# Weight sums in DRAM through one queue, squares on another engine: a one-core encoder layer on Trainium2

## The chip, the cores and the metric

The kernel runs on one core of a Trainium2 chip. A core has five engines that run side by side, each with its own instruction queue in order: TensorE (PE, matrix products; its weight loads appear as PEld), VectorE (DVE), ScalarE (ACT), GpSimd (POOL) and SyncE (SP). Transfers between DRAM and the on-chip memory, or within DRAM, are run by 16 DMA engines that all queues share. SP issues them through a queue that the profile calls q1 (hardware_dynamic), GpSimd through q0 (software_dynamic); a transfer that adds to what is at its destination ("accumulate") goes through GpSimd here. The metric is the time of one execution in microseconds (us) of device time; lower is better.

## The reference

One layer of a bidirectional encoder on x of 512 tokens by 1024 channels, in float32. First comes token mixing: RMSNorm, one wide input projection whose columns feed a two-way Mamba-2 scan, windowed attention and two gates; the branches are merged and projected, normed and added. Then comes channel mixing, the part that the change touches:

```python
h = rmsnorm(x, pre_mlp_norm[l])
f = jnp.square(jax.nn.relu(h @ w_mlp_in[l])) @ w_mlp_out[l]
x = x + rmsnorm(f, post_mlp_norm[l])
```

w_mlp_in is 1024 by 4096 and w_mlp_out 4096 by 1024.

## The kernel before, in words

Every float32 operand is split in two: hi, which ScalarE rounds to TensorE's faster float32 format (a CAST), and lo, the rest, which VectorE or GpSimd subtracts. A product is then three matmuls (mm3, line 418, recorded at line 412). Splits of weights are at line 492 (ScalarE) and 500 (VectorE or GpSimd) for most weights, at 1766 and 1770 for w_mlp_out and w_o; of activations at 429 to 433.

The work is a list of quanta, each a set of matmuls with the weights that it needs. The input projections, scan and attention take the first 629 us or so, the scan's output projection and the mixing until 756, the MLP the rest. The hidden width of 4096 is cut into four parts of 1024. Part 0 of the up projection is a plain product (up_halves, up_quantum). Then the down projection of part p (7 quanta) is interleaved with the up projection of part p + 1 (16 quanta); part 3 of the down projection comes last. Down part 0 starts at 803.8 us, part 1 at 885, part 2 at 969 and part 3 at 1051.9.

The up projections of parts 1 to 3 and all four down projections are folded: a 2 by 2 block product with seven block products instead of eight, after Strassen and Winograd. That needs four sums of blocks on each side. On the side of the weights they are made in one of two ways:

- **By transfer** (sums_in_dram, line 1451): a block is copied to a scratch tensor in DRAM and other blocks are accumulated on it, in eight transfers of 1 MB (four copies and four accumulations, copy after accumulation where one sum starts from another). Before the change the copies are issued by SP (line 1462) and the accumulations by GpSimd (line 1460). SUMS (line 41) says which parts do this and when: a first quantum and a pace in quanta. The numbers from 80 up count from 100 at the start of the MLP. Up parts 1, 2 and 3 (scratch up1s, up2s, up3s) are made during the scan, down parts 2 and 3 (dn2s, dn3s) during the MLP. The weights then come in finished: 28 loads of 256 KB for a down part.
- **On the core** (fold, lines 1737 to 1745): the down projection loads 16 raw blocks of 256 KB and VectorE makes the sums, 16 additions of 128x512 (lines 1728 and 1729). Down parts 0 and 1 do this.

The up projection's output is squared after a relu, by square (line 1570), 48 times in parts 1 to 3 (four products in four units of each part): ScalarE takes the relu into a tile r or q (line 1572), and VectorE multiplies max(a, 0), or min(a, 0), with it (line 1573). Where the folded product has the opposite sign, relu is taken of -a and the result is the negative of the square; combine (line 1646), which makes the operands of the down projection, takes that sign into account through its argument.

The order of the instructions on each engine is fixed when the program is made, by the class Planner: a model of the engines with a cost for each instruction (duration, line 210) and a due time worked back from the matmul that needs it (deadlines, line 245). It takes the ready instruction that is due first. For transfers it assumes 1 us of GpSimd for an issue, 125 bytes per ns on GpSimd's queue, and loads that are 1.6 times slower while that queue is busy (SOFT and SLOW, line 39). The transfers of the sums are also held back until the matmul issued before them in the program has started (held_back, line 1364). SP and GpSimd run their instructions in the planned order: if one waits, all behind it on that engine wait too.

Of the kernel before, what the change touches and what calls it, by code (L numbers as in the profile page):

```python
# [12 lines left out]
AF = mybir.ActivationFunctionType  # L13
ALU = mybir.AluOpType
# [23 lines left out]
HEADS = dict(scores=0, flip=2, values=3.5)  # L38
SOFT, SLOW = 125, 1.6
FETCH, STAGE, HALF = 2, 1, 3  # L40
SUMS = dict(up={1: (10, 2), 2: (26, 2), 3: (42, 2)}, down={2:(104,3),3:(130,3)})
BUCKET_STARTS = (1, 2, 3, 4, 5, 6, 7, 8, 12, 16, 23, 32, 46, 64, 91)


# [16 lines left out]
class Slots:  # L61
# [5 lines left out]
    def get(self, name, shape=(128, 512), dtype=F32):  # L67
        s = self.free.popleft()
        self.n += 1
        t = self.pool.tile(list(shape), dtype, tag=f"s{s}", name=f"{name}_{self.n}", bufs=1)  # L70
        self.tags[t.tensor.name] = f"s{s}", 1
        self.slot[id(t)] = (s, t)
        return t

    def put(self, *tiles):
        for t in tiles:
            self.free.append(self.slot.pop(id(t))[0])
# [275 lines left out]
class Trunk:  # L353
# [1097 lines left out]
    def sums_in_dram(self, name, src, q, pace):  # L1451

        nc = self.nc
        t = [self.dp.tile([512, 512], F32, name=f"{name}s{i}") for i in range(1, 5)]

        def step(out, a, plus):
            def run():
                a_ = t[a] if isinstance(a, int) else src(*a)
                if plus:
                    nc.gpsimd.dma_start(t[out], a_, accum_op=ALU.add)  # L1460
                else:
                    nc.sync.dma_start(t[out], a_)
            return run

        steps = [(0, (0, 0), False), (0, (0, 1), True), (2, (0, 1), False), (2, (1, 1), True),
                 (1, 0, False), (1, (1, 1), True), (3, 1, False), (3, (1, 0), True)]
        for i, args in enumerate(steps):
            self.at(q + pace * i, lambda fn=step(*args): self.held_back(fn))
        return t
# [77 lines left out]
    def up_unit(self, part, k):  # L1547

        nc = self.nc
        get, put = self.slots.get, self.slots.put  # L1550
        lo, hi = slice(0, 256), slice(256, 512)
        bank, made = {}, {}

        def block(n):
            return self.ups[part][n][:, k * 128:(k + 1) * 128].rearrange("(k p) n -> p k n", p=128)

        def product(w, b, at, first):
            ps, cols = bank[at[0]], at[1]
            for i in range(4):
                self.mm3(ps[:, cols], (w[0][:, i], w[1][:, i]), self.bt[b][i], first and i == 0, i == 3, not first)  # L1560

        def copy(n, at):
            made[n] = get(n, (128, 256))
            nc.scalar.copy(made[n], bank[at[0]][:, at[1]])

        def plus(at, a, n):
            nc.vector.tensor_tensor(bank[at[0]][:, at[1]], bank[a[0]][:, a[1]], made[n], op=ALU.add)
            put(made.pop(n))

        def square(at, r, side, dst=None):  # L1570
            a, cols = bank[at[0]], at[1]
            nc.scalar.activation(r[:, cols], a[:, cols], AF.Relu, scale=1.0 if side == ALU.max else -1.0)
            nc.vector.scalar_tensor_tensor((dst or a)[:, cols], a[:, cols], 0.0, r[:, cols], op0=side, op1=ALU.mult)
            if side == ALU.min:
                put(r)

        X, Y, Z, V = (1, lo), (0, hi), (0, lo), (1, hi)

        def one(w):
            bank[1] = self.bank("pp")  # L1580
            product(w[0], "B11", X, True)
            copy("c0", X)
            bank[0] = self.bank("pp")
            product(w[1], "T1", Y, True)
            copy("cy", Y)

        def two(w):
            product(w[0], "T2", X, False)
            copy("c1", X)
            product(w[1], "B21", Z, False)  # L1590
            plus(Z, Z, "c0")
            made["r"] = get("r")
            square(Z, made["r"], ALU.max)
            self.operand(part, k, bank[0][:, lo])

        def three(w):
            product(w[0], "T3", X, False)
            plus(V, X, "cy")
            square(V, get("q"), ALU.min)
            product(w[1], "B22", Y, False)  # L1600
            plus(Y, Y, "c1")
            square(Y, made["r"], ALU.max, made["r"])

        def four(w):
            product(w[0], "T4", X, False)
            square(X, get("q"), ALU.min)
            self.pair = [bank[0][:, lo], made["r"][:, hi], made["r"], bank[1]]
            self.combine(part, k, -1.0)

        def quantum(names, run, eng):  # L1610
            def go(parts):
                h, l = parts[0]
                run([(h[:, 4 * j:4 * j + 4], l[:, 4 * j:4 * j + 4]) for j in range(len(names))])
            return Quantum([([block(n) for n in names], 4 * len(names), 128, eng)], go)

        return [quantum(("A11", "S1"), one, UP_LO[0]), quantum(("S2", "A12"), two, UP_LO[1]),
                quantum(("S3", "S4"), three, UP_LO[2]), quantum(("A22",), four, UP_LO[3])]

    def up_done(self, ps, i):
# [23 lines left out]
        f["A12"] = self.halves(self.f12)[k % 2]  # L1643
        self.held[part].extend([{"A22": fa}] + [{"A12": self.f12}] * (k % 2))

    def combine(self, part, k, sign=None):

        nc = self.nc
        get, put = self.slots.get, self.slots.put
        a11, a21, r, b = self.pair  # L1650
        self.pair = []
        f = self.f[part, k]
        lo, hi = slice(0, 256), slice(256, 512)
        tt = nc.vector.tensor_tensor
        s, t = get("fs"), get("ft")
        fs, ft = self.twin("fs"), self.twin("ft")
        if sign is None:
            self.operand(part, k, a11)
            tt(t[:, lo], a21, b[:, hi], op=ALU.subtract)
        else:  # L1660
            tt(t[:, lo], a21, b[:, hi], op=ALU.add)
        tt(s[:, lo], t[:, lo], a11, op=ALU.subtract)
        tt(s[:, hi], a11, a21, op=ALU.subtract)
        put(r)
        self.split(*fs, s)
        if sign is None:
            tt(t[:, hi], b[:, lo], s[:, lo], op=ALU.add)
        else:
            tt(t[:, hi], s[:, lo], b[:, lo], op=ALU.subtract)
        self.split(*f["A22"], b[:, hi], sign)  # L1670
        self.split(*ft, t)
        self.split(*f["A12"], b[:, lo], sign)
        put(s, t)
        (f["S2"], f["S3"]), (f["S1"], f["S4"]) = self.halves(fs), self.halves(ft)
        self.held[part].extend([{"S3": fs}, {"S4": ft}])
# [181 lines left out]
    def build(self):  # L1857
# [11 lines left out]
        self.ups, self.dnt = {}, {}  # L1869
        for p, at in SUMS["up"].items():  # L1870
            if at[0] < 80:
# [35 lines left out]
        self.at(n() + 3, self.token_sums)  # L1907
        for p, at in SUMS["up"].items():
            if at[0] >= 80:
                self.ups[p] = self.up_blocks(p, n() + at[0] - 100, at[1])  # L1910
        for p, at in SUMS["down"].items():
            self.dnt[p] = self.down_sums(p, n() + at[0] - 100, at[1])
# [44 lines left out]
```

## Time and profile before

| | |
|---|---|
| median of 3 runs | 1100.24 us (1099.0 to 1104.58) |
| the profiled execution's own time | 1103.85 us |
| its span, first to last instruction | 1101.6 us |
| mean granted clock of TensorE | 0.993 |
| instructions | 18311 |

The times are those of whole executions; the profile is of one more execution, whose span of 1101.6 us lies within its own time of 1103.85 us. A row of the profile names a line of the program, the engine, the operation, the tile that is written and those that are read, the shapes and the count, and then the busy time in us and the mean duration of one in ns. After a second bar stand the idle time of that engine just before these instructions and what ended it. "SPq" is SP's queue of transfers, "POOLq" GpSimd's. A row of the chain of waits gives a start, a length and what the end of the program was waiting for at that time. A row of waits gives who waited for whom: the sum in us, how many times, and the longest.

### The profile page before, as it was taken

What the parts mean: (1) busy time and instruction counts of PE and PEld (TensorE: products, weight loads), DVE (VectorE), ACT (ScalarE), POOL (GpSimd) and SP (SyncE); (2) the same over time, 40 slices, a digit from 0 to 9 for tenths busy, and PEclk for the clock granted to TensorE, in tenths of its full rate; (3) what the DMA queues carried; (4) which work ended last, traced back from release to release, by engine and by line L of the source; (5) the groups of instructions that cost most, each with busy time, mean ns of one, the idle gap of its engine ahead of it and who ended that gap; (6) DMA issues with size and microseconds to landing.
All of it is one profiled execution on the core that took longest, in us unless ns stands there. A gap on an engine that the chain in (4) does not pass through costs nothing.

```text
span 1101.6 us, 18311 instructions
## 1 busy us (share of the span) xinstructions
PE 1074.3 (98%) x6016; PEld 915.6 (83%) x6016; DVE 838.7 (76%) x1471; ACT 695.3 (63%) x1515; POOL 814.4 (74%) x1003
## 2 busy tenths in 40 slices
PE   8999999999899999999999999999999999999997
PEld 7888888888778888888888888888888888988885
DVE  6568678699388687788778457769999798756867
ACT  5567676686577767576777522477867555646653
POOL 4447567568467799999898777666989888858753
PEclk9999999999989999999999999999999999999999
DMA  7458739868758776966664479844767599697673
GB/s 221 124 139 223 187 87 230 199 173 211 182 127 221 183 228 151 257 157 185 179 150 107 125 244 315 262 154 136 228 162 183 176 281 266 170 253 214 195 223 116
DMA packets 260016, 209.98 MB, mean 191 GB/s; under 512 B 14478, under 2 KB 214646, under 8 KB 259761
## 3 DMA queue, kind: packets, MB, share of 16 engines
q1 hardware_dynamic: 249212, 187.77, 58.5%
q0 software_dynamic: 10560, 20.97, 11.6%
q8 instruction: 47, 0.77, 0.3%
q14 instruction: 49, 0.39, 0.1%
q10 hardware_dynamic: 148, 0.07, 0.0%
HBM read 195.86 MB, written 54.85 MB: 228 GB/s over the span
## 4 chain that ended last, share of the span: by engine, by line
PE 61%; DVE 9%; DMA 3%; ACT 3%; issue 2%; SPq 1%; POOL 0%; POOLq 0%; DVEq 0%; ACTq 0%
PE pp L412 44%; PE ps L412 16%; DMA wd<-dn2s 2%; DVE wd L1729 1%; DMA rf<-csT 1%; PE ps L416 1%; DVE wl L500 1%; DMA wd<-in_w_mlp_out 1%; DVE fsl L430 1%; DVE acc L1816 1%; ACT P L887 0%; DVE wt L1728 0%; DVE ftl L430 0%; ACT m L1136 0%; DVE P L893 0%
## 5 line engine op out<-in xcount | busy, mean ns | idle before, releaser
L500 POOL TENSOR_TENSOR wl<-wr,wh 128x256 fp32r<-128x256 f32 (+1 forms) x503 | 427.4, 882 | 137.4 <-ACT wh L492 128.4
L412 PE MATMUL pp<-b,wh 128*128 128x512 f32 (+1 forms) x1840 | 519.3, 366 | 4.7 <-DVE fal L430 2.5
L412 PEld LDWEIGHTS pp<-b,wh 128*128 128x128 f32 x1840 | 330.3, 189 | 62.1 <-DVE fal L430 3.5
L412 PE MATMUL pp<-b,wl 128*128 128x512 f32 (+1 forms) x920 | 336.8, 366 | 1.3 <-DVE wl L500 1.3
L492 ACT CAST wh<-wr 128x1024 fp32r<-128x1024 f32 (+1 forms) x155 | 156.5, 1009 | 80.6 <-PE pp L412 46.6
L412 PEld LDWEIGHTS pp<-b,wl 128*128 128x128 f32 x920 | 173.7, 189 | 29.8 <-DVE wl L500 1.9
L1770 POOL TENSOR_TENSOR wl<-wd,wh 128x256 fp32r<-128x256 f32 x168 | 140.2, 863 | 49.6 <-ACT wh L1766 27.8
L1766 ACT CAST wh<-wd 128x512 fp32r<-128x512 f32 x124 | 72.6, 618 | 40.9 <-PE ps L412 13.0
L500 DVE TENSOR_TENSOR wl<-wr,wh 128x256 fp32r<-128x256 f32 x78 | 56.8, 744 | 9.4 <-ACT wh L492 9.1
L1135 ACT ACTIVATE n<-cb,tables 128x128 f32<-128x128 f32 x128 | 49.9, 392 | 19.9 <-DVE cb L1126 19.3
L967 DVE SCALAR_TENSOR_TENSOR u<-pp,cv,u 128x510 f32<-128x510 f32 (+1 forms) x64 | 47.7, 746 | 13.3 <-ACT u L963 11.9
L1136 ACT ACTIVATE m<-cb,tables 128x128 f32<-128x128 f32 x128 | 49.7, 391 | 1.2 <-DVE cb L1126 1.2
L1131 ACT ACTIVATE rf<-rf,tables 128x128 f32<-128x128 f32 x128 | 41.9, 393 | 13.4 <-DMA rf<-csT 13.0
L1171 POOL TENSOR_TENSOR w<-w,E 128x256 f32<-128x256 f32 x48 | 39.6, 840 | 7.1 <-DVE w L1167 5.9
L887 ACT ACTIVATE P<-P,mx 128x384 f32<-128x384 f32 (+1 forms) x64 | 35.2, 552 | 13.8 <-DVE mx L884 13.8
L1065 POOL TENSOR_TENSOR xd<-x,tables 128x256 f32<-128x256 f32 x48 | 33.9, 729 | 12.9 <-ACT x L990 12.2
L1129 POOL TENSOR_TENSOR rb<-rb,tables 128x512 f32<-128x512 f32 x32 | 34.2, 1075 | 12.0 <-DMA rb<-csT 8.6
L1816 DVE TENSOR_TENSOR acc<-acc,ps 128x512 f32<-128x512 f32 (+1 forms) x49 | 32.6, 668 | 12.2 <-PE ps L412 12.2
L878 DVE CUSTOM_DVE_ANT_0 P<-ps,bt,sink 128x256 f32<-128x256 f32 (+1 forms) x64 | 31.9, 545 | 10.4 <-PE ps L412 9.9
L1770 DVE TENSOR_TENSOR wl<-wd,wh 128x512 fp32r<-128x512 f32 x40 | 31.6, 797 | 10.3 <-ACT wh L1766 9.2
L1095 POOL TENSOR_TENSOR pv<-pv,tables 128x256 f32<-128x256 f32 x32 | 24.5, 778 | 16.6 <-DVE pv L1096 10.3
L1132 DVE TENSOR_TENSOR rf<-rf,rb 128x512 f32<-128x512 f32 x32 | 31.0, 970 | 4.4 <-POOL rb L1129 4.4
(338 smaller groups left out, 2503.8 us busy)
## 6 DMA issues: line engine op xcount, KB each, us to landing
wr<-in_w_in SPq DMA_DIRECT2D x74, 512.0 KB, 5.1
wd<-in_w_mlp_out SPq DMA_DIRECT2D x56, 256.0 KB, 5.0
wr<-in_w_mlp_in SPq DMA_DIRECT2D x36, 256.0 KB, 4.1
rb<-csT SPq DMA_DIRECT2D x32, 256.0 KB, 5.7
rf<-csT SPq DMA_DIRECT2D x32, 256.0 KB, 6.8
wr<-in_w_ssd_out SPq DMA_DIRECT2D x14, 512.0 KB, 4.8
wd<-in_w_o SPq DMA_DIRECT2D x28, 256.0 KB, 5.6
E<-csE SPq DMA_DIRECT2D x96, 64.0 KB, 4.4
```

The lines of the kernel that those rows point to most:

```text
L412: self.nc.tensor.matmul(out, lhsT, rhs, start=start, stop=stop, skip_group_check=more)
L492: self.nc.scalar.copy(hi[:, :m], raw)
L500: engines[e].tensor_tensor(lo[:, c], raw[:, c], hi[:, c].bitcast(F32), op=ALU.subtract)
L887: nc.scalar.activation(p[:, :w], p[:, :w], AF.Exp, bias=mx[:, n:n + 1], accum_out=sm[:, n:n + 1])
L967: nc.vector.scalar_tensor_tensor(u[:, a:e], ps[:, a + d:e + d], self.wtap(t, b), u[:, a:e], op0=ALU.mult, op1=ALU.add)
L1131: nc.scalar.activation(v4(rf)[:, h], v4(rf)[:, h], AF.Identity, bias=ncs[:, 0, h:h + 1])
L1135: nc.scalar.activation(v4(n)[:, h], cb[:, 0], AF.Copy, scale=dt[:, 0, h:h + 1])
L1136: nc.scalar.activation(v4(m)[:, h], cb[:, 1], AF.Copy, scale=dt[:, 1, h:h + 1])
L1171: nc.gpsimd.tensor_tensor(wc, wc, E[:, d], op=ALU.add)
L1766: nc.scalar.copy(hi, w)
L1770: (nc.vector if e == "v" else nc.gpsimd).tensor_tensor(low[:, q], w[:, q], hi[:, q].bitcast(F32), op=ALU.subtract)
L1816: self.nc.vector.tensor_tensor(self.acc[t, j][:, c], self.acc[t, j][:, c], ps[:, c], op=ALU.subtract if minus else ALU.add)
```

## The change

Four things are changed. The copies of sums_in_dram are issued by GpSimd, like the accumulations. The sums of up part 3 are made at the start of the MLP and not during the scan, and down part 2 makes its sums on the core, so that four sets of eight transfers are left of five. The squares are a relu and a Square, both on ScalarE. All squares are now positive, so the sign in combine goes away.

```diff
-SUMS = dict(up={1: (10, 2), 2: (26, 2), 3: (42, 2)}, down={2:(104,3),3:(130,3)})
+SUMS = dict(up={1: (10, 2), 2: (26, 2), 3: (102, 3)}, down={3:(130,3)})
...
         def step(out, a, plus):
             def run():
                 a_ = t[a] if isinstance(a, int) else src(*a)
-                if plus:
-                    nc.gpsimd.dma_start(t[out], a_, accum_op=ALU.add)
-                else:
-                    nc.sync.dma_start(t[out], a_)
+                nc.gpsimd.dma_start(t[out], a_, **(dict(accum_op=ALU.add) if plus else {}))
             return run
...
-        def square(at, r, side, dst=None):
+        def square(at, r, scale, dst=None):
             a, cols = bank[at[0]], at[1]
-            nc.scalar.activation(r[:, cols], a[:, cols], AF.Relu, scale=1.0 if side == ALU.max else -1.0)
-            nc.vector.scalar_tensor_tensor((dst or a)[:, cols], a[:, cols], 0.0, r[:, cols], op0=side, op1=ALU.mult)
-            if side == ALU.min:
+            nc.scalar.activation(r[:, cols], a[:, cols], AF.Relu, scale=scale)
+            nc.scalar.activation((dst or a)[:, cols], r[:, cols], AF.Square)
+            if scale < 0:
                 put(r)
...
-            square(Z, made["r"], ALU.max)
+            square(Z, made["r"], 1.0)
...
-            square(V, get("q"), ALU.min)
+            square(V, get("q"), -1.0)
...
-            square(Y, made["r"], ALU.max, made["r"])
+            square(Y, made["r"], 1.0, made["r"])
...
-            square(X, get("q"), ALU.min)
+            square(X, get("q"), -1.0)
             self.pair = [bank[0][:, lo], made["r"][:, hi], made["r"], bank[1]]
-            self.combine(part, k, -1.0)
+            self.combine(part, k, False)
...
-    def combine(self, part, k, sign=None):
+    def combine(self, part, k, whole=True):
...
-        if sign is None:
+        if whole:
             self.operand(part, k, a11)
-            tt(t[:, lo], a21, b[:, hi], op=ALU.subtract)
-        else:
-            tt(t[:, lo], a21, b[:, hi], op=ALU.add)
+        tt(t[:, lo], a21, b[:, hi], op=ALU.subtract)
...
-        if sign is None:
-            tt(t[:, hi], b[:, lo], s[:, lo], op=ALU.add)
-        else:
-            tt(t[:, hi], s[:, lo], b[:, lo], op=ALU.subtract)
-        self.split(*f["A22"], b[:, hi], sign)
+        tt(t[:, hi], b[:, lo], s[:, lo], op=ALU.add)
+        self.split(*f["A22"], b[:, hi])
         self.split(*ft, t)
-        self.split(*f["A12"], b[:, lo], sign)
+        self.split(*f["A12"], b[:, lo])
```

## The prediction

> **What bounds the kernel now.** I read the head of the page first, then busy time by stage, then the chain of waits, then the DMA queues. The head says whose time this is.
>
> ```profile
> span 1101.6 us, 18311 instructions
> PE 1074.3 (98%) x6016; PEld 915.6 (83%) x6016; DVE 838.7 (76%) x1471; ACT 695.3 (63%) x1515; POOL 814.4 (74%) x1003
> ```
>
> TensorE is idle for 1101.6 - 1074.3 = 27.3 us in all. The change leaves every matmul as it is, so 27.3 us is the most that it can win, and what it can lose is new idle time of TensorE. The windows view, with one row for a stretch (PE, PEld, DVE, ACT, POOL busy, then granted clock, DMA share, GB/s), shows where the idle time lies.
>
> ```profile
> core 0: us, PE busy (x) PEld busy (x) DVE busy (x) ACT busy (x) POOL busy (x), PEclk, DMA share, GB/s
> 0.00:50.00 50.00, 46.65 (x252) 39.38 (x253) 30.65 (x61) 27.73 (x55) 21.56 (x37) 1.00 0.64 181
> 250.00:350.00 100.00, 94.91 (x575) 79.31 (x574) 73.00 (x158) 63.77 (x156) 65.57 (x85) 0.97 0.72 180
> 803.80:885.00 81.20, 78.59 (x481) 70.44 (x480) 70.83 (x110) 50.26 (x95) 72.40 (x87) 0.98 0.64 179
> 885.00:969.00 84.00, 80.78 (x506) 71.55 (x505) 69.72 (x126) 47.03 (x92) 69.69 (x81) 1.00 0.94 242
> 969.00:1052.00 83.00, 79.58 (x508) 71.98 (x507) 59.70 (x113) 49.84 (x97) 60.32 (x74) 1.00 0.69 204
> 1075.00:1101.60 26.60, 18.49 (x92) 15.45 (x90) 20.19 (x39) 10.16 (x26) 10.38 (x12) 0.90 0.29 108
> 336.00:500.00 164.00, 164.00 (x891) 136.79 (x890) 128.04 (x189) 115.93 (x268) 147.25 (x179) 1.00 0.78 201
> ```
>
> The first 50 us and the tail hold 3.3 + 8.1 us; no edit is there. Parts 0, 1 and 2 of the MLP (the rows that begin at 803.8, 885 and 969) hold 2.6 + 3.2 + 3.4 = 9.2 us, and 250 to 350 holds 5.1 us plus a granted clock of 0.97, which is 3 us more. From 336 to 500, where the third up sum is made today, there is no idle time. So about 17 us are within reach, and one question decides: what made TensorE wait at 250 to 350 and in the MLP? The chain of waits names loads, and TensorE's own waits name little else.
>
> ```profile
> 284.14 9.66 DMA rf<-csT
> ...
> 961.79 7.10 DMA wd<-dn2s
> ...
> 981.89 10.78 DMA wd<-dn2s
> ...
> PE ps L416 <- DVE P L893: 4.0, 3, 3.3
> ...
> PE pp L412 <- DVE pp L1573: 2.2, 2, 1.2
> PE pp L412 <- ACT c L1564: 1.6, 1, 1.6
> PE pp L412 <- DVE wl L500: 1.3, 2, 1.1
> ...
> PE ps L412 <- POOL wl L1770: 0.6, 1, 0.6
> ```
>
> The wait of 4.0 us on P follows the slow load of rf. What ran beside the slow loads is in the list of the accumulating transfers on GpSimd's queue, and in windows over them.
>
> ```profile
> L1460 POOL DMA_DIRECT2D up2s<-in_w_mlp_in x4: 989/1033/1113, 215.0 to 324.8; - x4
> L1460 POOL DMA_DIRECT2D dn2s<-in_w_mlp_out x4: 989/1042/1138, 797.5 to 913.4; - x4
> L1460 POOL DMA_DIRECT2D dn3s<-in_w_mlp_out x4: 982/992/1009, 892.9 to 977.8; - x4
> DMA to landing us min/median/max: 10.0/11.8/13.6
> ...
> 281.00:288.00 7.00, 7.00 (x39) 6.11 (x38) 2.56 (x9) 2.60 (x5) 4.01 (x6) 1.00 1.04 178
> ...
> 979.00:986.00 7.00, 7.00 (x55) 6.74 (x55) 5.99 (x10) 4.63 (x9) 6.01 (x7) 1.00 0.95 143
> 988.00:993.00 5.00, 3.82 (x23) 3.27 (x22) 0.68 (x2) 1.19 (x3) 0.91 (x2) 1.00 1.11 347
> ```
>
> The last dn3 sum is issued at 977.8. From 979 to 986 the 16 DMA engines are full (0.95) but move only 143 GB/s: 1.0 MB in 7 us, which is that one transfer of 1 MB and hardly a load beside it. When it is over they move 347 GB/s, and TensorE pays: 3.82 busy of 5. **A transfer on GpSimd's queue takes the loads' bandwidth while it lasts**, more than the 1.6 that the planner allows for (SLOW, line 39). The window from 281, at 178 GB/s with a share of 1.04, is of the same kind and lies under the load of rf.
>
> **The change part by part.**
>
> *Copies on GpSimd's queue.* Today 40 transfers of 1 MB make five sums: 20 accumulations on GpSimd and 20 copies on SP. After it, four sums: 16 accumulations and 16 copies, all 32 on GpSimd. The prices of the two queues:
>
> ```profile
> q1 hardware_dynamic: 249212, 187.77, 58.5%
> q0 software_dynamic: 10560, 20.97, 11.6%
> DMA to landing us min/median/max: 5.8/8.3/10.5
> ```
>
> q0 is GpSimd's: 11.6% of 1101.6 us is 128 us of all 16 engines, 6.4 us for each of 20 transfers. q1 is SP's: 644 us for 187.77 MB, so 3.6 us for a copy of 1.05 MB. The losses that I charge to q0 are 250 to 350 (5.1 + 3) and part 2 (3.4): 11.5 us per 128 us, or 0.09 us for each microsecond that q0 runs. After the change it runs 16 x 6.4 = 102 us with accumulations, plus 16 copies whose price there no row shows. At q1's price they add 58 us, at the accumulation's 102. That is 32 to 77 us more than today: +2.9 to +6.9 us. Against it, loads that stood behind a copy in SP's own queue are free: at most 20 x 3.6 = 72 us at the same 0.09, or -6.5 us, so the bounds are -3.6 and +6.9. I take **+6.9**: the accumulation is the nearest row (same queue, same bytes), and all three slow loads on the chain lie beside an accumulation, none behind a copy. On SP the 20 issues end (median landing 8.3 us, from the row above); SP is not on the chain with them, so that is worth nothing.
>
> *GpSimd's own time.* An issue holds it for 1.04 us (rows of L1460). In the MLP 8 issues become 16: +8.3 us. Up to 300 us it gains 8 copies and it loses 4 accumulations after 336; there its slack hides them. In parts 0 and 1 it has 8.8 + 14.3 = 23.1 us idle; 14.8 would be left. Behind a copy in GpSimd's queue stand the splits of the weights (wl, lines 500 and 1770), and TensorE waits for those; a copy that reads an earlier sum also waits up to 13.6 us for it to land, with the splits behind it, if the planner puts it too early. Bounds 0 and +8.3. TensorE's waits on splits are 0.6 + 1.3 = 1.9 us today; scaled by 23.1/14.8 they are 3.0. I take **+1.1**.
>
> *Squares on ScalarE.*
>
> ```profile
> sum 352.00, DVE 19.99; mean DVE 1.54
> ...
> L1572 ACT ACTIVATE q<-pp 128x256 f32<-128x256 f32 x24 | 9.2, 384 | 11.0 <-DVE pp L1567 9.2 <-PE pp L412 1.2
> L1834 ACT ACTIVATE junk<-acc 128x256 f32<-128x256 f32 x2 | 0.8, 418 | 2.0 <-DVE acc L1816 2.0
> ```
>
> The first row is the sum of line 1573 over the MLP: 48 products on VectorE, 20.0 us. They become 48 Square instructions on ScalarE, at 418 ns (a square of that width) 20.1 us. ScalarE goes from 147.1 busy of 248.2 in parts 0 to 2 to about 165. TensorE's 2.2 us on line 1573 can go; its 1.6 us on ScalarE's copies (line 1564) can double, since casts and copies now queue behind squares. Bounds -2.2 and +1.6; I take **-1**. The plain sign in combine swaps instructions of one kind for others of the same width: nothing. The Trainium skill (ScalarE: Activation LUTs, Rules for kernel authors) speaks against this edit: it sends relu, max and mul to VectorE and budgets some 0.3 us plus 0.83 ns an element for an ACTIVATE. By it the squares would cost 48 x 0.51 = 24.5 us, 4.4 more; the trace's 418 ns does not bear that out.
>
> *Part 2 of the down projection makes its own sums.*
>
> ```profile
> L1729 DVE TENSOR_TENSOR wd<-wd,wd 128x512 f32<-128x512 f32 x16 | 13.6, 885 | 0.0
> L1728 DVE TENSOR_TENSOR wt<-wd,wd 128x512 f32<-128x512 f32 x8 | 8.0, 1016 | 0.6 <-POOL wl L1770 0.6
> L1729 DVE TENSOR_TENSOR wt<-wd,wd 128x512 f32<-128x512 f32 x8 | 6.7, 862 | 1.9 <-DMA wd<-in_w_mlp_out 1.9
> ```
>
> These 32 additions serve parts 0 and 1, so part 2 gets 16: (13.6 + 8.0 + 6.7)/2 = 14.2 us on VectorE, less its 16 squares (6.7). Its 59.7 of 83 become 67.2, less than parts 0 and 1 carry today. Loads fall from 28 to 16 of 256 KB, but the 16 are wanted in the first half, where the staged loads were late. Parts 0 and 1 do it this way with 2.6 and 3.2 us idle against 3.4. Bounds -3.4 (all of it) and +3.2 (a second part 1); I take **-0.5**.
>
> *The third up sum moves* from 336 to 500 into the slot that dn2 leaves (773 to 914). Where it was, TensorE has no idle time: nothing to win; where it goes, it stands in for dn2: nothing to lose, unless it is late (below).
>
> Sum: 6.9 + 1.1 - 1 - 0.5 = **+6.5 us**, a span of 1108.1 us. The profiled run took 1103.85 us, 3.6 above the median of 1100.24; I add 6.5 to the median: **1107 us**. This case's own range is 1103 to 1113.
>
> **The rivals.**
>
> *Only the issue moves.* All queues share the 16 engines, which are full in the bad windows either way (0.95 to 1.11); a copy is worth the same bytes on q0 as on q1, and q1's credit (-6.5) cancels the charge. What is left is 1.1 - 1 - 0.5 = -0.4: 1100 us, 1096 to 1105 with the other bounds. Against it: 143 GB/s beside q0 and 347 after it. The Trainium skill states this rival (DMA: Bandwidth & Descriptors, Issuing engines are not separate DMA queues): DMAs interleave on the same engines whoever starts them, and another issuer saves only issue time. The trace agrees on the engines and differs on the speed, as those two windows show.
>
> *Faster: the accumulation at 279 leaves the load of rf.* Its copy now goes through another queue and lands at another time, and the accumulation moves with it. If q0 is quiet between 284 and 294, the load takes its usual time, TensorE's 5.1 us and the lost clock (3 us) go, and with -0.4 the time is 1092 (1088 to 1095). It decides from a shift of about 8 us, the width of the slow window. For it: one collision makes a third of the loss within reach. Against it: the other 31 transfers shift too, and can land on other loads.
>
> *The third up sum is late.* Its four copies and four accumulations all queue behind splits on GpSimd. The last dn2 accumulation went out at 913.4 and lands by 927; the first load of up3 is issued at 961. From an issue later than 949 SP stands still with all loads behind it, and each microsecond is one of TensorE's: 1112 to 1122 us.
>
> ```profile
> 961.19 0.50 SPq L470 DMA_DIRECT2D wr<-up3s  x1
> ```
>
> **How the numbers follow.** The forecast 0.42, only issue 0.30, faster 0.18, late sum 0.10. A measurement of this kernel can tell about 0.5%, 5.5 us: below 1094.7 is faster, above 1105.7 slower. Faster is that rival and the rim of the second, 0.20. Within is 0.28 of the second and 0.05 from the forecast's lower end: 0.33. Slower is 0.37 and 0.10: 0.47. The range of 1092 to 1116 leaves out about half of the faster and half of the late cases. Both signs are likely, so the likeliest case's own range stands above.
>
> **What would show it.** Right: q0's share of the queues table rises from 11.6% towards 15 to 18%; loads beside its transfers take over 7 us on the chain; line 1573 vanishes from VectorE, and ScalarE gains some 20 us in the MLP; TensorE's idle time grows by 5 to 8 us in the MLP or up to 300 us. Wrong: a q0 copy at 3.6 us or less with the loads unharmed, or an undisturbed 250 to 350.

## The result, and the profile after

The changed kernel takes **1109.74 us** (median of 10 runs, 1104.92 to 1114.61) against 1101.43 us (10 runs, 1099.0 to 1108.65) for the kernel before on the same chip. The ratio is **1.0067, 95% interval [1.0038, 1.0096]**: slower, by 7.4 us in the middle of the interval (the medians lie 8.3 apart). Runs of one and the same kernel lie up to 10 us apart here, so one trace is one draw: the profiled execution of the changed kernel took 1113.59 us, 4 us above its median. Verdicts below therefore rest on the timed ratios, and traces are used for where things stand, above all where several show the same.

Page of the changed kernel: its span, busy times, and the two queues (packets, MB, share of 16 engines).

```profile
span 1111.7 us, 18284 instructions
...
PE 1077.5 (97%) x6016; PEld 918.9 (83%) x6016; DVE 843.7 (76%) x1439; ACT 713.5 (64%) x1563; POOL 824.4 (74%) x1015
...
q1 hardware_dynamic: 241884, 163.65, 51.9%
q0 software_dynamic: 10880, 33.56, 13.0%
```

TensorE's idle time is 1111.7 - 1077.5 = 34.2 us, 6.9 more than before. q0 carried 33.56 MB, 60% more than before, and yet its share rose only from 11.6 to 13.0%. For q0 the engines ran 0.13 x 1111.7 = 144.5 us. The windows view of the changed kernel says where the idle time is; the three long rows that begin at 802, 884 and 978 are parts 0, 1 and 2 of the MLP (columns as in the prediction).

```profile
core 0: us, PE busy (x) PEld busy (x) DVE busy (x) ACT busy (x) POOL busy (x), PEclk, DMA share, GB/s
250.00:350.00 100.00, 97.16 (x611) 82.22 (x610) 85.11 (x167) 69.11 (x171) 73.54 (x94) 1.00 0.73 178
...
802.00:884.00 82.00, 78.47 (x482) 69.17 (x482) 69.75 (x100) 54.35 (x107) 73.84 (x92) 1.00 0.65 183
884.00:978.00 94.00, 82.97 (x506) 74.02 (x505) 72.15 (x114) 55.00 (x112) 74.30 (x88) 0.96 0.77 203
978.00:1061.60 83.60, 80.90 (x507) 73.00 (x507) 66.36 (x108) 54.01 (x108) 64.27 (x74) 0.98 0.64 178
...
955.00:959.20 4.20, 4.20 (x31) 3.93 (x30) 2.42 (x5) 3.72 (x8) 3.94 (x6) 1.00 1.06 347
959.20:974.40 15.20, 10.03 (x66) 8.90 (x64) 12.86 (x17) 4.83 (x10) 7.94 (x9) 1.00 1.08 246
974.40:980.00 5.60, 4.59 (x17) 4.20 (x18) 1.45 (x3) 3.75 (x9) 2.80 (x4) 0.50 1.09 328
```

Two things happened. From 250 to 350, TensorE's idle time fell from 5.1 to 2.8 us and the granted clock rose from 0.97 to 1.00. Part 1 of the MLP, with the same 506 matmuls, grew from 84 to 94 us: 11.0 us idle instead of 3.2, at a clock of 0.96. Some 5.2 us of that lie in one stretch, 959.2 to 974.4, and behind it the clock is granted at 0.50. From 959.2 to 974.4 the DMA engines are full (1.08) and move 246 GB/s; in the 4 us before, they moved 347. The chain of waits of the changed kernel names what stands there.

```profile
915.41 8.62 DMA wd<-in_w_mlp_out
...
954.92 0.70 POOL wl L1762
955.62 0.93 POOL up3s L1459
956.56 0.50 POOL dn3s L1459
...
957.32 0.61 POOL wl L500
...
958.26 0.93 POOL wl L500
...
959.21 15.19 DMA wr<-in_w_mlp_in
```

Read it downwards. GpSimd finishes a split at 955.6, then issues two transfers, the last accumulation of up3 and a copy of dn3, and then makes the split (957.32, 958.26) that sets a buffer free. (The first half of that split had also waited for ScalarE's cast, which ended at 957.24, so the two issues need not have held it up.) SP loads into that buffer at once (959.21), and this load of 256 KB takes 15.19 us. At 959.13 GpSimd issues a third transfer, an accumulation of dn3. The queues table of 959.2 to 974.4 alone (packets, MB, share) says who has the engines meanwhile: GpSimd's queue.

```profile
q0 software_dynamic: 958, 2.91, 85.6%
q1 hardware_dynamic: 943, 0.80, 21.3%
```

TensorE's own waits show what it cost: the cast of that load, and the copy c behind it on ScalarE.

```profile
PE pp L412 <- ACT c L1561: 8.9, 4, 6.1
```

What GpSimd issued, from the view by tile of dn3s in the changed kernel (ns min/median/max, first and last start):

```profile
L1459 POOL DMA_DIRECT2D dn3s<-in_w_mlp_out x6: 862/1022/1043, 891.5 to 1041.6; - x6
L1459 POOL DMA_DIRECT2D dn3s<-dn3s x2: 539/692/846, 956.2 to 1010.8; - x2
```

The last accumulation of dn3 goes out at 1041.6; before, it was 977.8. The chain of eight steps is 64 us later at its end.

### The profile page after: what moved, and what is told of

Same layout as the page of the kernel before. It is cut to its first block, busy times and chain, and to the rows that moved or that the text cites. A ratio compares the mean times of both kernels' runs of the same rounds, so it can differ in the third digit from the quotient of the medians.

```text
span 1111.7 us, 18284 instructions
## 1 busy us (share of the span) xinstructions
PE 1077.5 (97%) x6016; PEld 918.9 (83%) x6016; DVE 843.7 (76%) x1439; ACT 713.5 (64%) x1563; POOL 824.4 (74%) x1015
## 3 DMA queue, kind: packets, MB, share of 16 engines
q0 software_dynamic: 10880, 33.56, 13.0%
## 4 chain that ended last, share of the span: by engine, by line
PE 78%; DVE 8%; DMA 6%; ACT 3%; issue 2%; POOL 2%; SPq 0%; POOLq 0%; DVEq 0%; ACTq 0%
PE pp L412 55%; PE ps L412 21%; PE ps L416 2%; DMA wr<-in_w_mlp_in 2%; DMA rf<-csT 2%; DVE wl L500 1%; DMA x1d<-x 1%; DVE wd L1721 1%; DMA wd<-in_w_mlp_out 1%; ACT wh L492 1%; POOL wl L1762 1%; DVE fsl L430 1%; POOL wl L500 1%; DMA wr<-in_w_in 0%; DVE u L967 0%
## 5 line engine op out<-in xcount | busy, mean ns | idle before, releaser
L1762 POOL TENSOR_TENSOR wl<-wd,wh 128x256 fp32r<-128x256 f32 x156 | 134.5, 901 | 33.3 <-ACT wh L1758 15.4
L1758 ACT CAST wh<-wd 128x512 fp32r<-128x512 f32 x116 | 67.9, 619 | 35.8 <-PE ps L412 14.6
L500 DVE TENSOR_TENSOR wl<-wr,wh 128x256 fp32r<-128x256 f32 x78 | 60.7, 808 | 9.1 <-ACT wh L492 8.3
L1762 POOL TENSOR_TENSOR wl<-wt,wh 128x256 fp32r<-128x256 f32 x40 | 36.0, 936 | 6.1 <-issue 3.5
```

What stands on the lines that cost most here:

```text
L500: engines[e].tensor_tensor(lo[:, c], raw[:, c], hi[:, c].bitcast(F32), op=ALU.subtract)
L1758: nc.scalar.copy(hi, w)
L1762: (nc.vector if e == "v" else nc.gpsimd).tensor_tensor(low[:, q], w[:, q], hi[:, q].bitcast(F32), op=ALU.subtract)
```

## The experiments

All ratios are to the kernel before, timed on the same chip in the same rounds. An overview first; "MLP" and "scan" say where copies stand on GpSimd.

| kernel | copies on GpSimd | median us (runs) | ratio [95%] |
|---|---|---|---|
| the change | scan and MLP | 1109.74 (10) | 1.0067 [1.0038, 1.0096] |
| e1_copies_on_sp | none | 1106.68 (12) | 1.0020 [1.0003, 1.0037] |
| e2_only_copies | scan and MLP | 1112.91 (7) | 1.0068 [1.0040, 1.0095] |
| e3_only_squares | none | 1103.63 (12) | 1.0001 [0.9981, 1.0021] |
| e4_only_sums | none | 1106.05 (12) | 0.9999 [0.9980, 1.0018] |
| e5_scan_copies_squares | scan | 1105.47 (12) | 1.0001 [0.9975, 1.0027] |
| e6_tiny_issue | none; 16 rows again, after SP's copy | 1115.62 (6) | 1.0105 [1.0074, 1.0136] |
| e7_plan_price | scan and MLP | 1118.68 (6) | 1.0141 [1.0107, 1.0175] |
| e9_due_earlier | scan and MLP | 1109.88 (12) | 1.0064 [1.0038, 1.0089] |
| e10_rows_split | MLP, 16 of 512 rows | 1106.43 (12) | 1.0013 [0.9994, 1.0031] |
| e12_copies_on_act | scan; MLP on ScalarE's queue | 1106.07 (12) | 1.0005 [0.9982, 1.0028] |
| e13_mlp_copies_on_sp | scan | 1104.53 (12) | 1.0006 [0.9979, 1.0032] |
| e14_fewer_in_mlp | scan and MLP, 4 instead of 8 in the MLP | 1111.44 (10) | 1.0069 [1.0043, 1.0095] |

The kernels before, as timed beside them: 1105.47 us (e1 to e4), 1103.79 (e5 to e9) and 1105.47 (e10 to e14).

### Which part of the change: e1 to e4

**e1**, the changed kernel with its copies back on SP:

```diff
-                nc.gpsimd.dma_start(t[out], a_, **(dict(accum_op=ALU.add) if plus else {}))
+                if plus:
+                    nc.gpsimd.dma_start(t[out], a_, accum_op=ALU.add)
+                else:
+                    nc.sync.dma_start(t[out], a_)
```

> The changed kernel, with the copies of the sums given back to SP; squares and schedule of the sums as changed. Theory A (the copies on GpSimd are the loss: they are issued late among its splits, and the transfers of q0 come in clusters that take the loads' bandwidth): 1100 to 1104 us, and no load of more than 11 us on the chain of waits in part 1. Theory B (the squares on ScalarE are the loss) and theory C (the third up sum in the MLP is the loss): 1107 to 1111 us, as the changed kernel.

**e2**, the kernel before with nothing but the copies on GpSimd (the same edit the other way round; five sums, 20 copies):

> The kernel before, with its copies issued by GpSimd and nothing else changed (five sums, squares on VectorE). Theory A: 1106 to 1112 us, since 20 copies join 20 accumulations on q0. B and C: 1099 to 1103 us.

**e3**, the kernel before with nothing but the squares on ScalarE:

```diff
-            nc.vector.scalar_tensor_tensor((dst or a)[:, cols], a[:, cols], 0.0, r[:, cols], op0=side, op1=ALU.mult)
+            nc.scalar.activation((dst or a)[:, cols], r[:, cols], AF.Square)
```

> The kernel before, with the squares on ScalarE (and the plain sign in combine) and nothing else changed. Theory B: 1106 to 1111 us, with ScalarE's copies c (line 1564) as what TensorE waits for. A and C: 1098 to 1103 us; by the prediction's own term (-1 us), 1100.

**e4**, the kernel before with nothing but the new schedule of the sums:

```diff
-SUMS = dict(up={1: (10, 2), 2: (26, 2), 3: (42, 2)}, down={2:(104,3),3:(130,3)})
+SUMS = dict(up={1: (10, 2), 2: (26, 2), 3: (102, 3)}, down={3:(130,3)})
```

> The kernel before, with the schedule of the sums as changed (third up sum at the start of the MLP, down part 2 makes its sums on the core) and nothing else. Theory C: 1105 to 1111 us. A and B: 1098 to 1103 us.

Measured: e2 alone is as slow as the whole change (1.0068 against 1.0067); squares alone (1.0001) and schedule alone (0.9999) are each nothing within 0.2%. Without the copies, the rest is at 1.0020, whose interval just leaves out 1; that the two harmless parts together may cost 2 us is not explained here. So the copies on GpSimd carry most of the loss: 0.68% where they are added alone, 20 of them (e2), and 1.0067 - 1.0020, some 0.5%, where the 16 of the change are taken away (e1).

Theory A's sign in the trace failed all the same. It expected no load of more than 11 us on the chain in part 1 of e1. There is one of 13.68 us, with a stretch over it in which TensorE is idle for 5.5 of 14 us. That is as much as in the bad stretch of the changed kernel, and GpSimd's queue has the engines to the same share, with accumulations alone (issued at 909.2, 912.2 and 918.5):

```profile
915.88 13.68 DMA wd<-in_w_mlp_out
```

```profile
916.00:930.00 14.00, 8.51 (x58) 7.70 (x57) 4.97 (x10) 4.14 (x8) 5.01 (x7) 0.91 1.11 221
```

```profile
q0 software_dynamic: 1072, 2.13, 84.2%
```

The traces of e3, e5 and e13 have such a load there too (13.02, 13.15 and 12.83 us), and none of these kernels is above 1.0020. One load of 13 to 15 us and a stall of 5 us are therefore not the mark of copies on GpSimd's queue.

The page of e1 also gives the price of an accumulation without copies beside it on its queue:

```profile
q0 software_dynamic: 8448, 16.78, 9.2%
```

9.2% of its span of 1104.5 us is 101.6 us for 16 accumulations, 6.35 us each. In the changed kernel the same 16 leave 144.5 - 101.6 = 42.9 us for 16 copies: **2.7 us for a copy on q0**.

### Where: scan or MLP: e5 and e13

**e5**, the kernel before with the squares on ScalarE and with the copies on GpSimd in the scan only (there `self.now` is below 80). **e13**, the changed kernel with the copies of the MLP back on SP:

```diff
-                nc.gpsimd.dma_start(t[out], a_, **(dict(accum_op=ALU.add) if plus else {}))
+                if plus:
+                    nc.gpsimd.dma_start(t[out], a_, accum_op=ALU.add)
+                else:
+                    (nc.gpsimd if self.now < 80 else nc.sync).dma_start(t[out], a_)
```

> The kernel before, with the squares on ScalarE and with only the copies of the scan (parts 1 to 3 of the up projection, up to about 330 us) on GpSimd; the copies of the MLP stay on SP. Theory 'place' (a copy on GpSimd's queue loses in the MLP, where it lands beside loads that TensorE needs soon, and wins in the scan, where the accumulation near 279 us leaves the load of rf): the scan ends 2 to 3 us earlier than before, parts 0 to 2 as before, a ratio of 0.996 to 0.999. Theory 'every copy' (each q0 copy loses about the same, 0.3 us each of 20): 12 of 20 copies give 4 us, a ratio of 1.002 to 1.005.

> The changed kernel with only the 8 copies of the MLP back on SP. By the sum of the stages: the scan of the changed kernel (626 us against 629 to 631) and the MLP of the kernel with all copies on SP (parts 0 to 2: 249.6): about 4 us less than that kernel, a ratio of 0.996 to 1.000. If the scan's 3 us was chance and not the copies on GpSimd: 1.000 to 1.003.

With 12 copies on GpSimd in the scan (e5) and with 8 (e13) nothing is lost: 1.0001 and 1.0006. The loss is in the MLP. The cleanest comparison is that of the changed kernel (1.0067) with e13 (1.0006) and, below, e12 (1.0005): they differ from it by the queue of the eight MLP copies, and by what the planner makes of that, and their intervals do not touch its own. The gain expected of the scan is seen in a trace but isn't large enough to be timed: e5 came out above its range for 'place', and e13 in the range that it gave to chance. The chain of waits and the windows of e13:

```profile
276.22 9.19 DMA rf<-csT
```

```profile
250.00:350.00 100.00, 98.63 (x622) 83.33 (x621) 87.53 (x170) 70.96 (x173) 74.43 (x94) 1.00 0.71 178
...
953.00:970.00 17.00, 16.59 (x111) 15.20 (x110) 13.77 (x23) 11.70 (x25) 13.28 (x16) 1.00 1.11 312
```

and the chain of e1, with the copies of the scan on SP:

```profile
281.60 12.53 DMA rf<-csT
```

These are two different loads of rf: SP issues them at 272.5 and 281.6 in e1 and at 276.2 and 287.7 in e13, and the accumulation that goes out at 279.2 in e1, between the two, goes out at 273.3 in e13, ahead of both (before: 278.9; the changed kernel: 271.5). The slow load is then the earlier of the two, and still takes 9 us, but TensorE pays less for it: its idle time from 250 to 350 is 1.4 us in e13 and was 5.1 before. Timed, e13 against e1 is 0.14% (1.5 us) with intervals of 0.2 to 0.3%: not told from zero. The last window above, of e13, is the one to compare with the changed kernel's 959.2 to 974.4: the engines are as full (1.11), but they move 312 GB/s, and TensorE is idle for 0.4 us of 17. A single accumulation (953.3) stands beside the loads there, against two and a copy in the changed kernel. Two things limit the comparison: this execution of e13 was the fastest of its twelve, and its own bad stretch lies earlier, from 911 to 924 (4.7 us idle at 224 GB/s).

### What of a copy costs: e6, e10, e12

**e6**, the copies on SP, and after each copy of the MLP a GpSimd transfer of its first 16 rows once more, which waits for SP's copy to land, as the accumulation then waits for both. **e10**, each copy of the MLP cut in two that don't wait for each other, and the copies of the scan on SP. **e12**, the copies of the MLP on ScalarE's queue.

```diff
                 else:
                     nc.sync.dma_start(t[out], a_)
+                    if self.now >= 80:                                  # e6
+                        nc.gpsimd.dma_start(t[out][:16], a_[:16])
...
+                    nc.sync.dma_start(t[out][16:], a_[16:])             # e10, MLP
+                    nc.gpsimd.dma_start(t[out][:16], a_[:16])
...
+                    (nc.gpsimd if self.now < 80 else nc.scalar).dma_start(t[out], a_)   # e12
```

> The changed kernel with its copies back on SP, and after each copy of the MLP a GpSimd transfer of its first 16 rows (the same bytes once more). The data volume of q0 is as with copies on SP; GpSimd's issues, their order in its queue and the splits behind them are nearly those of the changed kernel. Theory 'bytes' (the loads lose bandwidth beside 1 MB transfers on q0): as with all copies on SP, a ratio to before of 1.000 to 1.003, and no load over 12 us on the chain in part 1. Theory 'issue' (GpSimd's time and the order of its queue): as the changed kernel, 1.005 to 1.008.

> The changed kernel with the copies of the scan on SP, and with each copy of the MLP cut: rows 16 to 511 on SP, rows 0 to 15 (32 KB) on GpSimd, neither waiting for the other. GpSimd issues as often as in the changed kernel and its splits stand behind as many transfers, but q0 carries 8 x 1.02 MB less. Theory 'issue' (what a transfer costs GpSimd and the splits behind it): a ratio of 1.005 to 1.010, as with the tiny transfers that waited for SP's copies (1.0105). Theory 'bytes' (bandwidth that 1 MB on q0 takes from the loads): 1.000 to 1.003, as with all copies on SP (1.002), and the 1.0105 came from the wait for SP's copies.

> The changed kernel with the 8 copies of the MLP on ScalarE's DMA queue; those of the scan stay on GpSimd. Theory 'GpSimd' (its issue or its queue is what costs): the MLP as with copies on SP, the scan as in the changed kernel, together a ratio of 0.996 to 1.001, unless ScalarE's own issues (8 in the MLP) delay its casts. Theory 'SP alone is good' (only behind the loads in SP's own queue do copies keep out of the loads' way): 1.004 to 1.009.

After e6 alone (1.0105, above the ranges of both theories) "issue" looked nearer: a loss without the bytes. e10 takes that back: with as many issues on GpSimd in the MLP as the changed kernel, its copies being of 32 KB each there, the ratio is 1.0013, as with all copies on SP. What e6 has and e10 has not is the wait. The view by tile of dn3s, e6 and then e10:

```profile
L1460 POOL DMA_DIRECT2D dn3s<-in_w_mlp_out x4: 1015/1041/1382, 913.9 to 1042.5; - x4
```

```profile
L1460 POOL DMA_DIRECT2D dn3s<-in_w_mlp_out x4: 1032/1055/1439, 916.5 to 998.5; - x4
```

With each tiny transfer behind SP's copy and ahead of the accumulation, the chain of dn3 ends 44 us later than in e10, as late as in the changed kernel (1041.6), and the chain of waits of e6 has a slow load right beside that last accumulation:

```profile
1043.14 10.63 DMA wd<-in_w_mlp_out
```

That load cost little, though: from 1040 to 1060 TensorE is idle for 0.4 us in e6. What e6 does lose isn't in one place of its trace.

GpSimd's issue time as such costs nothing that can be seen (e10). And SP isn't special: on ScalarE's queue (e12, 1.0005) the copies do no harm either. It is GpSimd's queue that they must keep out of in the MLP. Two explanations offer themselves, and neither is shown. **Its bytes on q0** would fit e10 against the changed kernel, 1.0013 against 1.0067 with the same number of issues; e14 below speaks against them. **Lateness of the sum** would fit e6. Over all the kernels here, those above 1.005 issue the last accumulation of dn3 at 1001.7 or later in their traces and the others at 998.5 or earlier. But SP's loads of dn3s waited for that sum for 1.6 us in the changed kernel, for 3.9 us in e1, and not at all in e2, e7 and e14, which are slow. So a wait for the late sum isn't what costs there.

One thing speaks against too simple a picture. The profiled execution of e10 was the slowest of its twelve (1112.22 us), and it too has a bad stretch at that place:

```profile
960.00:976.00 16.00, 11.93 (x77) 10.63 (x76) 13.65 (x19) 7.19 (x16) 10.38 (x12) 1.00 1.07 226
```

Two accumulations had gone out at 960 and 961 there. Accumulations alone can do this too, as in e1. Whether copies on GpSimd make it more frequent can't be told from one trace of each kernel.

### How many, and when: e14, e9, e7

**e14**, the changed kernel with the third up sum back in the scan, `up={..., 3: (42, 2)}`, so that the MLP has the dn3 sum alone (4 copies, 4 accumulations). **e9**, transfers on GpSimd due 20 us ahead of their readers instead of 4. **e7**, the planner prices copies on q0 at 370 bytes per ns instead of 125:

```diff
-            c += 4000 if "DMA" in type(self.ins[n]).__name__ else 0
+            c += (20000 if e == "POOL" else 4000) if "DMA" in type(self.ins[n]).__name__ else 0    # e9
...
-                soft = max(soft, end + self.LEAD) + size / SOFT
+                soft = max(soft, end + self.LEAD) + size / (370 if self.ins[n].name in COPIES else SOFT)    # e7
```

> All copies on GpSimd as in the changed kernel, but the third up sum back in the scan (from quantum 42), so that the MLP has one sum: 8 transfers on GpSimd (4 copies, 4 accumulations), as many issues as in the kernel before and half of all transfers. Theory 'number' (the loss grows with GpSimd's issues in the MLP: 8 more cost about 7 us): the loss goes, a ratio of 0.995 to 1.001. Theory 'copy' (a copy on GpSimd costs where it lands, 8 cost 7 us): 4 cost 3 to 4 us in the MLP, 1.001 to 1.005. Theory 'kind' (any copy on GpSimd, in the scan too): 1.005 or more.

> The changed kernel, but transfers on GpSimd are due 20 us ahead of their first reader in the planner in place of 4, so that they go ahead of the splits of the weights. Theory 'clusters' (three transfers pile up behind splits and go out within 4 us, ahead of one load): the issues in part 1 spread, no load of 15 us is left at 959 us, part 1 is 84 to 88 us in place of 94, ratio to before 0.999 to 1.003. Theory 'bytes' (it is what q0 moves in all, wherever): still 1.004 to 1.009. Theory 'splits' (a transfer ahead of a split makes TensorE wait for the split): TensorE's waits on POOL grow from under 1 us to 3 to 6 us.

> The changed kernel, but the planner, which fills the queues, prices a copy on GpSimd's queue with 370 bytes per ns (about 2.8 us for 1 MB, what the traces show) in place of 125 (8.4 us). Theory 'price' (the planner holds q0 to be busy for longer than it is, and so issues late and in clusters): part 1 comes back to 83 to 87 us and the ratio to 0.999 to 1.003. Theory 'queue' (transfers wait for an idle gap of GpSimd, whatever the price): 1.004 to 1.009.

e14 was a miss for "number" and for "copy": half the transfers, and the whole loss (1.0069). "Kind" gave the right number for a wrong reason, since e5 and e13 have the copies of the scan for nothing. It narrows the place down: the four copies of dn3 seem to be enough. (e14 with these four on SP was not run; that its schedule costs nothing is taken from e4 and e5.) And it speaks against the bytes. From 760 us to the end, q0 carries as much in e14 as in the kernel before, and for less of the engines' time; first e14, then the kernel before:

```profile
q0 software_dynamic: 2720, 8.39, 10.8%
```

```profile
q0 software_dynamic: 4224, 8.39, 14.4%
```

The chains of e14, e9 and e7 show the same load, of in_w_mlp_in late in part 1, as in the changed kernel:

```profile
956.31 12.92 DMA wr<-in_w_mlp_in
```

```profile
959.53 14.72 DMA wr<-in_w_mlp_in
```

```profile
965.59 15.46 DMA wr<-in_w_mlp_in
```

In e14 a window over that load has the same signature as in the changed kernel, full engines that move less (258 GB/s) while TensorE is idle for 3.3 us:

```profile
956.30:969.20 12.90, 9.62 (x66) 8.75 (x64) 7.51 (x14) 4.76 (x10) 6.92 (x8) 1.00 1.08 258
```

e9 didn't do what it was made for: the three transfers still go out between 951 and 955, so it says nothing on "clusters", and its 1.0064 is the change once more. In e7 the copies are priced nearly as they run, and the kernel is the slowest of all (1.0141, above the ranges of both theories): mending the planner's price doesn't mend the loss. Why e7 is slower still wasn't followed up; in its trace the chain has that load too. In e2, which is as slow as the change, the load is missing: from 950 to 990 TensorE is idle for 2.5 us there, against 2.7 in the kernel before, and its extra idle time is spread over the MLP.

The planner made a new order for each of these kernels, so a single one could be slow because of its order. But all five with 1 MB copies on GpSimd in the MLP (the change, e2, e7, e9, e14) are at 1.0064 to 1.0141, and seven without them (e1, e3, e4, e5, e10, e12, e13) at 0.9999 to 1.0020; e6 is the one exception.

No version beats the kernel before by more than the measurement can tell; e13, whose profiled span of 1098.0 us was the shortest of all, has a median of 1104.53 and a ratio of 1.0006.

## Why the prediction came out

The forecast was 1107 us and +6.5 us; measured were 1109.74 us and +0.67%, or 7.4 us. The sum and its largest term come near; the working of that term does not hold, and that its number fits is luck. By the runs the split is also another one: some 5 us for the copies and 2 for the rest (e1, 1.0020), not 6.9 and -0.4.

- **Copies on GpSimd's queue, +6.9.** Alone they cost 0.68% (e2), 7.5 us, there with 20 copies; the 16 of the change cost some 5 us (against e1). But the step that gave it, "0.09 us for each microsecond that q0 runs", with a copy priced at the accumulation's 6.4 us, failed twice, in opposite directions. A copy takes 2.7 us on q0, so q0 ran 144.5 us and not 205, and 16.5 us more than before; at 0.09 that is 1.5 us. And the loss isn't spread over what q0 carries: copies in the scan cost nothing (e5, e13), and in the MLP a kernel with four is as slow as one with eight (e14). What sets the loss in the MLP is open (below). "A q0 copy at 3.6 us or less with the loads unharmed" was to prove it wrong: the first half came true; the load of 15.19 us stands beside q0's transfers, but e1 has one of 13.68 us without a copy there. Of the signs of being right, q0's share of 15 to 18% failed (13.0%). That TensorE would lose 5 to 8 us came in another form: 9.4 us more idle time in the MLP (from 760 on), 2.5 less up to 350.
- **GpSimd's own time, +1.1.** e10 has all the issues of the MLP and is at 1.0013, against 1.0020 with none: no cost. TensorE's waits on splits, 1.9 us before and 3.0 by the step, stand in no row of its waits in the changed kernel. The other half of that step, a copy that waits for an earlier sum to land, was mentioned and priced at part of 8.3 us; e6, which adds waits of GpSimd for SP's copies, lost 1.05%, 11.6 us, though what of e6 costs isn't shown.
- **Squares on ScalarE, -1,** and **part 2's own sums, -0.5.** Alone the squares are at 1.0001, the new schedule (with the third up sum) at 0.9999: both nothing that can be told, inside their bounds. A square took 389 ns at the median rather than 418 in 36 of 48, and ScalarE in parts 0 to 2 is busy for 54.35 + 55.00 + 54.01 = 163.4 us (165 were worked out).
- **The third up sum, 0.** It was late by the rival's own point: its last accumulation went out at 955.6, after 949. But SP did not stand still behind it; it was one of the transfers beside the slow load, and with this sum back in the scan the loss stays (e14). Where the step said "nothing to lose", it was right.
- **Rival: only the issue moves.** It holds in the scan and it holds for ScalarE's queue; in the MLP it falls (1.0067 against 1.0020). The Trainium skill (DMA: Bandwidth & Descriptors, Issuing engines are not separate DMA queues) says that transfers interleave on the same engines whoever issues them, and that spreading them saves issue time alone. The runs agree for SP and ScalarE (1.0020 and 1.0005) and differ for GpSimd (1.0067).
- **Rival: the accumulation at 279 leaves the load of rf.** In the traces this came about: the accumulation goes out 7 us earlier (271.5), the load that was slow is off the chain, another load of rf (276.2 in e13) takes the long time in its place, and TensorE's stall halves. It was given the price of the whole stall, 8 us; the traces show 2 to 4 us less idle time, and the MLP of the changed kernel starts 1.8 us earlier (802.0 against 803.8). The timed ratio of e13 can't tell it from nothing, and in the MLP more was lost.

**What stays open.** That the MLP copies on GpSimd's queue cause the loss is shown by timed kernels; how they do so is not. Each explanation has a kernel against it. The number of issues has e10. The bytes and the time of q0 have e14. The late end of the sum has e14, e7 and e2, where no load waits for it. The load near 959 us has e2, which is slow without it, and e1, e5 and e13, which have one like it at 911 to 916 and are not slow. What is left, and not tested, is which transfers and loads the planned order puts side by side: in the changed kernel, e9 and e7 an accumulation of up3, a copy and an accumulation of dn3 go out within 4 us. A kernel that starts the dn3 sum some quanta earlier was not tried, nor one with the order held fixed and only the queue of the copies changed.

## What to carry to other kernels

Don't price a transfer by its bytes or by its share of the time alone: eight copies on GpSimd's queue in the MLP cost some 0.5% here, eight to twelve in the scan nothing, and a rate per microsecond of the queue gave the right sum by luck. Where a chain of transfers alternates between two queues, moving all of it onto one busy engine saved nothing here and made its end late, 64 us in the trace. Before a slow load is called the cause, look for it in the kernels that are not slow: here they have one too. And before a cheap term is trusted, make it alone: the squares and the new schedule were each nothing, the copies most of the loss.

## What the runs showed of the hardware

- On GpSimd's queue a plain copy of 1 MB takes the 16 engines for 2.7 us (2.9 in e14) and an accumulation for 6.35 us, so the price is that of the operation. With eight copies of that kind, e13's page gives 0.112 x 1098.0 - 101.6 = 21.4 us, again 2.7 each. On ScalarE's queue, q10 in e12, eight copies take 0.021 x 1104.9 = 23.2 us, 2.9 each: the queue makes no difference to that price.

```profile
q0 software_dynamic: 9664, 25.17, 11.2%
```

```profile
q10 hardware_dynamic: 2388, 8.46, 2.1%
```

- The engines are full at very different speeds: a share of 1.08 at 246 GB/s in the changed kernel and of 1.11 at 221 in e1, with two or three accumulations issued in or just before the stretch, and of 1.11 at 312 in e13 with one. That fits the prices above: 1.05 MB in 6.35 us is 165 GB/s for an accumulation, in 2.7 us 390 for a copy. A share near 1 does not say that much is moved, and a low rate points to accumulations.
- After TensorE's stall of some 5 us the granted clock was 0.50 for the next 5.6 us in the changed kernel, and 0.50 for 6 us in e7 after a stall of 5.4, so that half of that stretch, some 3 us, is paid on top of the stall.
